# The delta net's triangular systems: substituted in two groups of eight instead of sixteen at once

## The chip, the cores and the metric

The kernel runs on one core of a Trainium2 chip. The metric is the device time of one execution in microseconds (us), the median of several runs. Five engines work side by side: TensorE (PE) multiplies matrices and transposes into PSUM, VectorE (DVE) and ScalarE (ACT) work element by element on SBUF and PSUM, GpSimd (POOL) on SBUF alone, and SyncE (SP) issues the loads.

## The reference, cut to what matters

The reference is a block with a mixer and a mixture of experts, and after it four layers: attention with forget gates, gated linear attention, the gated delta net, and attention again. The change is in the delta net, `gdn_mixer`, with 256 tokens, 8 value heads of 128, 4 key heads and chunks of 64 tokens:

```python
qkv = jax.nn.silu(causal_conv(qkv, conv_w))
q = l2_norm(q) * d ** -0.5; k = l2_norm(k)      # each repeated for two heads
...
tri = jnp.where(strict, (kb @ k.T) * decay, 0.0) + jnp.eye(64)
u = triangular_solve(tri, vb)
w = triangular_solve(tri, kb * exp(gc))
...   # then a scan over the chunks with u, w and the queries
```

For each head and chunk a unit lower triangular system of 64 has to be solved. The kernel makes the inverse of `tri` itself.

## The kernel before

**Layout.** Function `gdn` does the layer. Two chunks stand in one 128x128 tile, so 8 heads by 2 token tiles give 16 "systems" of 128x128; U (line 1526) holds their strict triangles. Four systems are worked on at a time, in a PSUM tile of 512 columns: group g4 = 0 to 3 has heads 2 g4 and 2 g4 + 1. Groups 0 and 1, the first eight systems, need key heads 0 and 1 (unit 2) and query unit 0; groups 2 and 3 need units 3 and 1.

**Units.** The columns of the input weights are taken in units of 256 (`unit`, line 1497: 2 and 3 keys, 0 and 1 queries, 4 to 7 values) and two for the gate z (2048, of 512 columns, and 2560). The raw weights, 1 MB a unit, are loaded into a ring of six buffers (pool `ring`, tag "w"); ACT rounds each half unit (line 247) and DVE takes the rest (line 248), so that a product is done in three passes, and PE does 48 matmuls for a unit (line 277; line 298 where tokens are the rows). The end of a dense product traces the load and the split of the next unit (`ahead`, line 261). The product stands in PSUM (pool `pd`, four tiles); `conv_silu` copies it into one buffer "pad" on DVE (352), multiplies by four taps on ACT (356) and DVE (360), and applies silu (363, 365). `l2` normalises keys and queries: squares on ACT, sums on PE (1510), the inverse root on POOL, transposes (1520), a multiply on DVE (1522). `systems` makes U from them (1550 to 1561).

**The inverse.** `compact` picks the 8x8 diagonal blocks of four systems into `own`. `substitute` inverts all of them by forward substitution: their coefficients are widened (1601: a part on ACT, a part on POOL) and transposed into PSUM (1604), and then seven rows are made one after another, each by a multiply and a reduce on DVE (1609, 1610) that read the coefficients from PSUM. The result is transposed back (1612), spread into block diagonal tiles T and, flipped by PE (1581), V = its transpose. Three levels of doubling (8 to 16, 32, 64) follow: `lower` multiplies U by T (1636) and masks it into X (1642), `update` multiplies X by V or V by X and adds (1654, 1655), `flipped` copies the flipped T into V (1660). In `update` the level decides which. One loop does the twelve steps (three levels by four groups) with a lag, so that four groups are under way.

**What sets the order.** A planner orders each engine's instructions when the kernel is built, by its own costs: of those ready it takes the one that is first in the program. `issue_after` adds an order on one engine alone. Two ties matter. `conv_silu` issues its copy into pad behind `made[2]`, the last reduce of the substitution, once that is set (line 1499); and `queries` (multiplies on the queries' tiles) behind the last lower step. A tag of a pool gives out a fixed number of buffers: 4 PSUM tiles "ps" for the work above, 4 "pd" for dense products, 2 "cv" for the results of the convolution, and 6 ring buffers "w", of which `zs` (line 1471, the gate z, written from line 1083 on) has one through the whole layer.

After the doubling come `rest`, `upper`, `across` and `lower_half` (1716 to 1736), which solve for the values chunk by chunk, and `result`.

Of the kernel before, what the change touches and what calls it, by code (L numbers as in the profile page):

```python
# [1461 lines left out]
def gdn(s, I, st, hT, cols):  # L1462
# [34 lines left out]
    def unit(u):  # L1497
        pq = first if u == 2 else s.dense(W, 0, 256 * u, T, st.x)
        return s.conv_silu(None, pq, rb2, lambda i, j: cw[:, 16 * j + 2 * u + i:16 * j + 2 * u + i + 1], after=made.get(2))
# [63 lines left out]

    k, q = unit(2), unit(0)
    gate_z(s, st, zs, 0, s.dense_tm(W, 2048, st.x))
    kn, qn = l2(k, q)
    k = unit(3)
    systems(0, kn, qn)
    q = unit(1)
    kn, qn = l2(k, q)  # L1570
    systems(1, kn, qn)

    def sys4(t, g4):
        return t[:, 4 * g4:4 * g4 + 4]
# [15 lines left out]

    def substitute():

        nc.vector.tensor_tensor(own, own, s.eye8[:, None, :].to_broadcast([P, 16, 8]), OP.add)
        t = s.tmp.tile([P, 16, 8], F32, tag="junk", name="rows8", bufs=1)
        nc.vector.tensor_copy(t, s.eye8[:, None, :].to_broadcast([P, 16, 8]))
        pts = [s.ps.tile([P, 512], F32, name="ps") for _ in range(2)]
        for c, n in enumerate((4, 3)):
            wide = s.tmp.tile([P, 4, 16, 8], F32, tag="kq"[c], name="wide")  # L1600
            (nc.scalar.copy, nc.gpsimd.tensor_copy)[c](
                wide[:, :n], own[:, :, 4 * c + 1:4 * c + 1 + n].rearrange("p a i -> p i a")[:, :, :, None].to_broadcast([P, n, 16, 8]))
            for i in range(n):
                nc.tensor.transpose(pts[c][:, i * P:(i + 1) * P], wide[:, i].rearrange("p a c -> p (a c)"), s.ident)
        for i in range(1, 8):
            at = (i - 1) % 4 * P
            m = pts[i // 5][:, at:at + P].rearrange("p (n j) -> p n j", j=8)[:, :, :i + 1]
            x = s.tmp.tile([P, 16, 8], F32, tag="E", name="terms")
            nc.vector.tensor_tensor(x[:, :, :i + 1], m, t[:, :, :i + 1], OP.mult)
            made[2] = nc.vector.tensor_reduce(t[:, :, i], x[:, :, :i + 1], AX.X, OP.add).ins  # L1610
        pt = s.ps.tile([P, 512], F32, name="ps")
        nc.tensor.transpose(pt[:, :P], t.rearrange("p n i -> p (n i)"), s.ident)
        nc.scalar.copy(own.rearrange("p a c -> p (a c)"), pt[:, :P])

# [7 lines left out]

    X, last = {}, [None]

    def halves(x, lev):

        x = x.rearrange("p a (n c) -> p a n c", c=16 << lev)
        return x[:, :, :, :8 << lev], x[:, :, :, 8 << lev:]

    def lower(i):  # L1630

        lev, g4 = divmod(i, 4)
        t = sys4(Tm, g4)
        pt = s.ps.tile([P, 512], F32, name="ps")
        for a in range(4):
            nc.tensor.matmul(pt[:, a * P:(a + 1) * P], U[:, 2 * g4 + a // 2, (a % 2) * P:(a % 2 + 1) * P], t[:, a],  # L1636
                             start=True, stop=True)
        X[i] = s.tmp.tile([P, 4, P], F32, tag="kq"[i % 2], name="X")
        xl, xr = halves(X[i], lev)
        nc.gpsimd.memset(xr, 0.0)  # L1640
        nb = P // (16 << lev)
        last[0] = nc.vector.tensor_tensor(
            xl, halves(pt.rearrange("p (a t) -> p a t", a=4), lev)[0],
                                s.below[:, lev, :nb][:, None, :, None].to_broadcast([P, 4, nb, 8 << lev]), OP.mult).ins

    def update(i):

        lev, g4 = divmod(i, 4)
        t, v, x = sys4(Tm, g4), sys4(Vm, g4), X[i]
        l, m, out, side = (v, x, t, 0) if lev < 2 else (x, v, v, 1)  # L1650
        out = halves(out, lev)[side]
        pt = s.ps.tile([P, 512], F32, name="ps")
        for a in range(4):
            nc.tensor.matmul(pt[:, a * P:(a + 1) * P], l[:, a], m[:, a], start=True, stop=True)  # L1654
        nc.vector.tensor_tensor(out, out, halves(pt.rearrange("p (a t) -> p a t", a=4), lev)[side], OP.add)

    def flipped(i):
        lev, g4 = divmod(i, 4)
        if lev < 2:
            nc.scalar.copy(halves(sys4(Vm, g4), lev)[1], halves(flip(sys4(Tm, g4)), lev)[1])  # L1660
# [13 lines left out]

    for g4 in range(4):
        compact(g4)
    substitute()
    v_dense(0)
    v_dense(1)
    for g4 in range(4):  # L1680
        spread(g4)
    v_turn(0)
    for i in range(12 + 3):
        if i < 12:
            lower(i)
        if 0 <= i - 2 < 12:
            update(i - 2)
        if 0 <= i - 3 < 12:
            flipped(i - 3)
        if i in (0, 5):  # L1690
            v_dense(2 + i // 5)
        if i in (3, 7, 10):
            v_turn((3, 7, 10).index(i) + 1)
        if i >= 4 and i < 12 and i % 2 == 0:
            with s.tc.issue_after(last[0]):
                queries((i - 4) // 2)

# [260 lines left out]
```

## Time and profile before

| what | value |
|---|---|
| median of three runs (lowest, highest) | 1293.36 us (1290.65, 1295.31) |
| the profiled execution: its own time, its span | 1291.23 us, 1289.6 us |
| PE, DVE, ACT busy, share of the span | 88%, 46%, 38% |
| delta net: first dense products about, substitution, end of the results | 970 us, 1050 to 1065 us, 1113 us |
| one split on DVE (line 248), mean | 1.22 us |

All times in rows are microseconds from the span's start; the page's engine shares are averages over stages that are bound in different ways. A busy time is from the start of an instruction to its end; a matmul starts while the one ahead of it is still in the pipeline, so the distance of starts is the price of one more. What a stage is limited by is read from the waits in it.

### The profile page before, as it was taken

Reading aid. Unit: us, or ns where it says so; the run is one execution under the profiler, and the core shown is the slowest. Engines: PE = TensorE matmul, PEld = TensorE weight load, DVE = VectorE, ACT = ScalarE, POOL = GpSimd, SP = SyncE. Lnnn points to the kernel's source line nnn. Section 1 sums busy time; section 2 is a strip of 40 time slices with the busy share of each in tenths; the row PEclk is TensorE's granted clock in tenths of the full one; section 3 lists DMA queues with packets and bytes.
Section 4 is the critical chain, followed back from the end, with each engine's and each line's share of the span. In section 5 each row is a group of like instructions: output and inputs, shape, how many; then the busy total and the mean of one; then the engine's idle time right before and its main releaser. Section 6 shows DMA issues by size and latency. Waiting matters only on the chain.

```text
span 1289.6 us, 18973 instructions
## 1 busy us (share of the span) xinstructions
PE 1134.1 (88%) x7458; PEld 845.0 (66%) x7459; DVE 589.9 (46%) x1136; ACT 491.4 (38%) x996; POOL 137.6 (11%) x406
## 2 busy tenths in 40 slices
PE   5999999996778677777777999999999969999998
PEld 4998999741323131322314788989688959897887
DVE  3976776410101010110104565757467777666554
ACT  4554454210101010000104567656455533356763
POOL 2000632000000000000000332010001110012310
PEclk8999999998899898999989999999999979999999
DMA  6843647799999999999999553454335420165620
GB/s 226 290 134 99 191 159 283 280 421 425 421 424 424 425 424 424 425 425 424 425 424 317 171 164 131 166 165 153 112 109 170 138 76 2 34 165 168 158 98 33
DMA packets 126903, 312.72 MB, mean 242 GB/s; under 512 B 7559, under 2 KB 72842, under 8 KB 109530
## 3 DMA queue, kind: packets, MB, share of 16 engines
q1 hardware_dynamic: 126458, 311.26, 65.5%
q8 instruction: 60, 0.98, 0.3%
q0 software_dynamic: 352, 0.20, 0.1%
q14 instruction: 33, 0.27, 0.1%
HBM read 310.39 MB, written 1.05 MB: 242 GB/s over the span
## 4 chain that ended last, share of the span: by engine, by line
PE 39%; DMA 25%; DVE 3%; ACT 2%; issue 1%; POOL 1%; SPq 0%; DVEq 0%; ACTq 0%
PE pd L298 19%; DMA we<-in_w_down 12%; PE pd L277 9%; DMA we<-in_w_gate 6%; DMA we<-in_w_up 6%; DMA w<-in_fox_w_in 2%; DVE wl L248 1%; PE ps L1654 1%; PE ps L1193 1%; PE ps L1581 1%; PE ps L1636 1%; ACT wh L247 1%; PE ps L1211 1%; PE pd L969 1%; DVE cv L360 0%
## 5 line engine op out<-in xcount | busy, mean ns | idle before, releaser
L277 PE MATMUL pd<-x,wh 128*128 128x256 f32 x1744 | 327.6, 288 | 2.3 <-DVE x L161 1.2
L248 DVE TENSOR_TENSOR wl<-w,wh 128x1024 fp32r<-128x1024 f32 (+1 forms) x206 | 251.2, 1223 | 119.0 <-ACT wh L247 117.6
L247 ACT CAST wh<-w 128x1024 fp32r<-128x1024 f32 (+1 forms) x206 | 214.5, 1046 | 203.2 <-PE pd L277 103.8
L277 PEld LDWEIGHTS pd<-x,wh 128*128 128x128 f32 x1744 | 276.7, 194 | 5.5 <-DVE x L161 2.1
L298 PE MATMUL pd<-wh,x 128*128 128x512 f32 (+3 forms) x896 | 249.5, 367 | 6.9 <-ACT x L160 2.4
L277 PE MATMUL pd<-x,wl 128*128 128x256 f32 x872 | 248.8, 287 | 0.8 <-DVE wl L248 0.8
L969 PE MATMUL pd<-we,xt 128*32 128x512 f32 x1012 | 173.2, 681 | 71.9 <-DMA we<-in_w_up 50.6
L298 PEld LDWEIGHTS pd<-wh,x 128*128 128x128 f32 x896 | 159.7, 190 | 33.8 <-ACT wh L247 3.8
L277 PEld LDWEIGHTS pd<-x,wl 128*128 128x128 f32 x872 | 168.7, 194 | 1.6 <-DVE wl L248 1.3
L969 PEld LDWEIGHTS pd<-we,xt 128*32 128x32 f32 x1012 | 40.5, 122 | 195.7 <-DMA we<-in_w_up 86.8
L298 PE MATMUL pd<-wl,x 128*128 128x512 f32 (+3 forms) x448 | 158.3, 366 | 1.5 <-DVE wl L248 1.4
L993 PE MATMUL pd<-we,sq 128*32 128x512 f32 x512 | 98.2, 624 | 27.6 <-DMA we<-in_w_down 21.7
L298 PEld LDWEIGHTS pd<-wl,x 128*128 128x128 f32 x448 | 84.2, 190 | 15.6 <-DVE wl L248 2.9
L1005 DVE TENSOR_TENSOR hT<-hT,ps 128x512 f32<-128x512 f32 x32 | 22.0, 687 | 149.3 <-PE ps L1004 149.3
L993 PEld LDWEIGHTS pd<-we,sq 128*32 128x32 f32 x512 | 24.7, 112 | 94.0 <-issue 45.0
L982 DVE SCALAR_TENSOR_TENSOR cv<-cv,rslot,pd 128x512 f32<-128x512 f32 x8 | 6.0, 747 | 130.9 <-PE pd L969 130.9
L99 POOL TENSOR_SCALAR rq_y<-rs_v 128x8 int32<-128x8 int32 (+2 forms) x24 | 6.4, 266 | 522.8 <-DVE rs_v L192 440.0
L987 ACT COPY sq<-ps 128x512 f32<-128x512 f32 x8 | 4.7, 585 | 149.8 <-PE ps L985 149.8
L999 ACT COPY ys<-pd 128x512 f32<-128x512 f32 x16 | 9.3, 586 | 120.7 <-PE pd L993 120.7
L1316 POOL MEMSET at<- 128x1024 f32 x1 | 1.0, 951 | 434.7 <-PE pd L993 434.7
L980 DVE SCALAR_TENSOR_TENSOR cv<-th,pd 128x512 f32<-128x512 f32 x8 | 5.5, 688 | 85.8 <-ACT th L978 85.8
L978 ACT ACTIVATE th<-pd,rslot 128x512 f32<-128x512 f32 x8 | 5.5, 687 | 90.3 <-PE pd L969 51.3
(492 smaller groups left out, 1374.3 us busy)
## 6 DMA issues: line engine op xcount, KB each, us to landing
we<-in_w_down SPq DMA_DIRECT2D x46, 1024.0 KB, 14.8
we<-in_w_up SPq DMA_DIRECT2D x45, 1024.0 KB, 16.0
we<-in_w_gate SPq DMA_DIRECT2D x43, 1024.0 KB, 14.5
w<-in_fox_w_in SPq DMA_DIRECT2D x30, 1024.0 KB, 6.8
w<-in_w_in SPq DMA_DIRECT2D x22, 1024.0 KB, 7.7
we<-in_w_up SPq DMA_DIRECT2D x38, 512.0 KB, 14.2
we<-in_w_down SPq DMA_DIRECT2D x36, 512.0 KB, 15.8
we<-in_w_gate SPq DMA_DIRECT2D x34, 512.0 KB, 15.6
```

The source lines that it names most:

```text
L247: nc.scalar.copy(h, v[:, k:k + m])
L248: nc.vector.tensor_tensor(l, v[:, k:k + m], h, OP.subtract)
L277: nc.tensor.matmul(acc[:, c], w[k][:, cs], x[:, k, p], start=start and c == 0 and at == 0 and i == 0, stop=stop and at == KC - 1 and i == ...
L298: nc.tensor.matmul(acc[j], x[:, k, p, ts], w[k], start=k == order[0] and i == 0 and (n != T or j == 0), stop=k == order[-1] and i == 2, sk ...
L969: mm = nc.tensor.matmul(out[32 * j:32 * j + 32], xt[:, k, 32 * j:32 * j + 32], w[name, 4 * q + j, k // 4][k % 4], start=k == 0, stop=k == ...
L993: mm = nc.tensor.matmul(py[h][32 * j:32 * j + 32], at[:, f, 32 * j:32 * j + 32], w["w_down", 4 * q + j, f // 2][f % 2][:, 512 * h:512 * h ...
L1005: nc.vector.tensor_tensor(hT[:, 2 * u:2 * u + 2], hT[:, 2 * u:2 * u + 2], pt.rearrange("p (i t) -> p i t", i=2), OP.add)
L1193: nc.tensor.transpose(pt[:, (2 * i + j) * P:(2 * i + j + 1) * P], n4[w, j][:, 2 * o + i], s.ident)
L1211: nc.tensor.matmul(pl[:, P:384], q[:, P:], k, start=False, stop=False, skip_group_check=True)
L1581: nc.tensor.transpose(pt[:, a * P:(a + 1) * P], x[:, a], s.ident)
L1636: nc.tensor.matmul(pt[:, a * P:(a + 1) * P], U[:, 2 * g4 + a // 2, (a % 2) * P:(a % 2 + 1) * P], t[:, a], start=True, stop=True)
L1654: nc.tensor.matmul(pt[:, a * P:(a + 1) * P], l[:, a], m[:, a], start=True, stop=True)
```

## The change

The sixteen systems are substituted eight at a time. `substitute(u)` takes one half of `own`, with 64 partitions (8 systems by 8 columns); ACT makes the whole wide copy, and ACT copies the transposed coefficients from PSUM into SBUF, from where the seven rows read them. The substitution of the first eight stands before unit 1 in the program, and the convolution of unit 1 is now behind its last reduce. The first eight are doubled, level by level with two groups in turn, after the second eight's substitution in the program and before its result is transposed back (`substituted`). The second eight follow in the same way, with the value units between. The buffers X of the doubling, which were in tags "k" and "q" for each step anew, are one tile of the ring "w" for the whole layer; a half of it also holds the wide copy and the coefficients of the substitution.

```diff
--- before.py
+++ after.py
@@ -1561,139 +1561,160 @@
+    room = s.ring.tile([P, KC * WIDE], F32, tag="w", name="X")[:, :2048].rearrange("p (u g a t) -> p u g a t", u=2, g=2, a=4)
+    X = [room[:, 0], room[:, 1]]
+    sys4x = lambda g4: X[g4 // 2][:, g4 % 2]
...
+    def substitute(u):
+
+        mine = own[:, 8 * u:8 * u + 8]
+        nc.vector.tensor_tensor(mine, mine, s.eye8[:, None, :].to_broadcast([P, 8, 8]), OP.add)
+        t = s.tmp.tile([64, 16, 8], F32, tag="junk", name="rows8", bufs=1)
+        nc.vector.tensor_copy(t, s.eye8[:64, None, :].to_broadcast([64, 16, 8]))
+        flat = X[u].rearrange("p g a t -> p (g a t)")
+        wide = flat[:, 576:].rearrange("p (i a c) -> p i a c", i=7, a=8)
+        nc.scalar.copy(wide, mine[:, :, 1:].rearrange("p a i -> p i a")[:, :, :, None].to_broadcast([P, 7, 8, 8]))
+        rows_of = lambda i: flat[:64, (i - 1) * P:i * P]
+        for at, n in ((0, 4), (4, 3)):
+            pt = s.ps.tile([P, 512], F32, name="ps")
+            for i in range(n):
+                nc.tensor.transpose(pt[:64, i * P:(i + 1) * P], wide[:, at + i].rearrange("p a c -> p (a c)"), s.ident)
+            nc.scalar.copy(flat[:64, at * P:(at + n) * P], pt[:64, :n * P])
+        for i in range(1, 8):
+            m = rows_of(i).rearrange("p (n j) -> p n j", j=8)[:, :, :i + 1]
+            x = s.tmp.tile([64, 16, 8], F32, tag="E", name="terms")
+            nc.vector.tensor_tensor(x[:, :, :i + 1], m, t[:, :, :i + 1], OP.mult)
+            made[2] = nc.vector.tensor_reduce(t[:, :, i], x[:, :, :i + 1], AX.X, OP.add).ins
+        return t
+
+    def substituted(u, t):
+        mine = own[:, 8 * u:8 * u + 8]
+        pt = s.ps.tile([P, 512], F32, name="ps")
+        nc.tensor.transpose(pt[:, :64], t.rearrange("p n i -> p (n i)"), s.ident[:64, :64])
+        nc.scalar.copy(mine.rearrange("p a c -> p (a c)"), pt[:, :64])
...
+    def lower(lev, g4):
+
+        t = sys4(Tm, g4)
...
+        xl, xr = halves(sys4x(g4), lev)
+        nc.gpsimd.memset(xr, 0.0)
+        nb = P // (16 << lev)
+        last[0] = nc.vector.tensor_tensor(
...
+    def update(lev, g4):
+
+        t, v, x = sys4(Tm, g4), sys4(Vm, g4), sys4x(g4)
...
+    def double(u, lev):
+        for step in (lower, update, flipped):
+            for g4 in (2 * u, 2 * u + 1):
+                step(lev, g4)
+
+    def pick(u):
+        compact(2 * u)
+        compact(2 * u + 1)
+
+    def end(u):
+        spread(2 * u)
+        spread(2 * u + 1)
     k, q = unit(2), unit(0)
     gate_z(s, st, zs, 0, s.dense_tm(W, 2048, st.x))
     kn, qn = l2(k, q)
     k = unit(3)
     systems(0, kn, qn)
+    pick(0)
+    t = substitute(0)
     q = unit(1)
+    substituted(0, t)
     kn, qn = l2(k, q)
+    end(0)
     systems(1, kn, qn)
...
-    def substitute():
-
-        nc.vector.tensor_tensor(own, own, s.eye8[:, None, :].to_broadcast([P, 16, 8]), OP.add)
-        t = s.tmp.tile([P, 16, 8], F32, tag="junk", name="rows8", bufs=1)
-        nc.vector.tensor_copy(t, s.eye8[:, None, :].to_broadcast([P, 16, 8]))
-        pts = [s.ps.tile([P, 512], F32, name="ps") for _ in range(2)]
-        for c, n in enumerate((4, 3)):
-            wide = s.tmp.tile([P, 4, 16, 8], F32, tag="kq"[c], name="wide")
-            (nc.scalar.copy, nc.gpsimd.tensor_copy)[c](
-                wide[:, :n], own[:, :, 4 * c + 1:4 * c + 1 + n].rearrange("p a i -> p i a")[:, :, :, None].to_broadcast([P, n, 16, 8]))
-            for i in range(n):
-                nc.tensor.transpose(pts[c][:, i * P:(i + 1) * P], wide[:, i].rearrange("p a c -> p (a c)"), s.ident)
-        for i in range(1, 8):
-            at = (i - 1) % 4 * P
-            m = pts[i // 5][:, at:at + P].rearrange("p (n j) -> p n j", j=8)[:, :, :i + 1]
-            x = s.tmp.tile([P, 16, 8], F32, tag="E", name="terms")
-            nc.vector.tensor_tensor(x[:, :, :i + 1], m, t[:, :, :i + 1], OP.mult)
-            made[2] = nc.vector.tensor_reduce(t[:, :, i], x[:, :, :i + 1], AX.X, OP.add).ins
-        pt = s.ps.tile([P, 512], F32, name="ps")
-        nc.tensor.transpose(pt[:, :P], t.rearrange("p n i -> p (n i)"), s.ident)
-        nc.scalar.copy(own.rearrange("p a c -> p (a c)"), pt[:, :P])
...
-    def lower(i):
-
-        lev, g4 = divmod(i, 4)
-        t = sys4(Tm, g4)
...
-        X[i] = s.tmp.tile([P, 4, P], F32, tag="kq"[i % 2], name="X")
-        xl, xr = halves(X[i], lev)
-        nc.gpsimd.memset(xr, 0.0)
...
-    def update(i):
-
-        lev, g4 = divmod(i, 4)
-        t, v, x = sys4(Tm, g4), sys4(Vm, g4), X[i]
...
-    for g4 in range(4):
-        compact(g4)
-    substitute()
+    pick(1)
+    t = substitute(1)
     v_dense(0)
+    for lev in range(3):
+        double(0, lev)
     v_dense(1)
-    for g4 in range(4):
-        spread(g4)
+    substituted(1, t)
     v_turn(0)
-    for i in range(12 + 3):
-        if i < 12:
-            lower(i)
-        if 0 <= i - 2 < 12:
-            update(i - 2)
-        if 0 <= i - 3 < 12:
-            flipped(i - 3)
-        if i in (0, 5):
-            v_dense(2 + i // 5)
-        if i in (3, 7, 10):
-            v_turn((3, 7, 10).index(i) + 1)
-        if i >= 4 and i < 12 and i % 2 == 0:
+    end(1)
+    double(1, 0)
+    v_dense(2)
+    v_turn(1)
+    for lev in (1, 2):
+        double(1, lev)
+        for g4 in (2 * lev - 2, 2 * lev - 1):
             with s.tc.issue_after(last[0]):
-                queries((i - 4) // 2)
+                queries(g4)
+        if lev == 1:
+            v_dense(3)
+            v_turn(2)
+    v_turn(3)
```

The functions `flip`, `compact`, `spread`, `halves`, `v_dense` and `v_turn` only move up, unchanged; `update` and `flipped` take level and group where they took a running number.

## Rows read from the trace of the kernel before

**Rows 1.** Waits of PE, 1000 to 1100: total us, times, longest us

```profile
PE ps L1604 <- ACT wide L1601: 4.9, 1, 4.9
PE ps L1612 <- DVE rows L1610: 3.3, 1, 3.3
PE ps L1672 <- DVE cv L365: 1.9, 1, 1.9
PE ps L1581 <- DVE TV L1618: 1.3, 1, 1.3
PE ps L1581 <- DVE TV L1655: 0.6, 1, 0.6
```

**Rows 2.** Timeline of PE: start us, us, instructions, count

```profile
1059.64 3.65 PE L1581 MATMUL ps<-ident,TV 128*128 128x128 f32 x16 [1.25 <-DVE TV L1618]
...
1065.71 2.84 PE L1636 MATMUL ps<-TV,U 128*128 128x128 f32 x24
...
1077.16 0.60 PE L1581 MATMUL ps<-ident,TV 128*128 128x128 f32 x4
1077.59 1.06 PE L1636 MATMUL ps<-TV,U 128*128 128x128 f32 x8
```

**Rows 3.** Stretches: length, busy us (instructions) of PE, PEld, DVE, ACT, POOL; clock, DMA share, GB/s

```profile
1009.70:1029.00 19.30, 19.30 (x155) 18.08 (x154) 16.61 (x33) 11.69 (x25) 0.91 (x3) 1.00 0.33 110
...
1041.30:1052.80 11.50, 6.31 (x42) 4.66 (x40) 9.22 (x18) 5.93 (x16) 0.55 (x2) 0.88 0.48 95
1052.80:1065.20 12.40, 5.88 (x24) 4.82 (x24) 10.25 (x28) 4.70 (x10) 1.08 (x4) 0.56 0.00 0
1065.20:1093.80 28.60, 27.84 (x246) 27.49 (x247) 23.13 (x63) 8.85 (x20) 2.49 (x8) 1.00 0.00 1
```

**Rows 4.** Timelines of ACT, DVE and SP's queue, 945 to 985

```profile
979.40 0.84 ACT L1082 ACTIVATE th<-pd,rh 128x256 f32<-128x256 f32 x2 [3.47 <-DVE gx L1477]
...
982.89 1.98 ACT L247 CAST wh<-w 128x1024 fp32r<-128x1024 f32 x2
...
979.90 0.79 DVE L1083 SCALAR_TENSOR_TENSOR zs<-th,pd 128x256 f32<-128x256 f32 x2 [0.27 <-ACT th L1082]
...
945.47 14.57 SPq L229 DMA_DIRECT2D w<-in_gdn_w_in  x3
```

**Rows 5.** Timeline of DVE, 1051 to 1064

```profile
1051.83 0.29 DVE L1595 TENSOR_TENSOR own<-own,eye 128x128 f32<-128x128 f32 x1
1053.98 0.19 DVE L1609 TENSOR_TENSOR terms<-ps,rows 128x32 f32<-128x32 f32 x1 [1.86 <-PE ps L1604]
...
1057.24 0.29 DVE L1609 TENSOR_TENSOR terms<-ps,rows 128x128 f32<-128x128 f32 x1
...
1057.77 0.68 DVE L352 TENSOR_TENSOR pad<-pd,rstd_b 128x512 f32<-128x512 f32 x1
...
1061.21 2.46 DVE L360 SCALAR_TENSOR_TENSOR cv<-pad,gconv_half,cv 128x256 f32<-128x256 f32 x6
```

**Rows 6.** Timeline of ACT, the wide copy

```profile
1052.15 0.62 ACT L1601 COPY wide<-own 128x512 f32<-128x512 f32 x1 [3.08 <-DVE own L1595]
```

**Rows 7.** Timeline of DVE, 1028 to 1043

```profile
1028.03 0.69 DVE L365 SCALAR_TENSOR_TENSOR cv<-th,cv 128x512 f32<-128x512 f32 x1
...
1033.01 1.22 DVE L248 TENSOR_TENSOR wl<-w,wh 128x1024 fp32r<-128x1024 f32 x1
1034.15 1.11 DVE L1591 TENSOR_REDUCE own<-sq 128x32 f32<-128x512 f32 x1
...
1041.94 0.69 DVE L1522 TENSOR_TENSOR k<-ps,cv 128x512 f32<-128x512 f32 x1 [1.13 <-PE ps L1520]
```

**Rows 8.** Groups of DVE, 1053 to 1092: count, busy us, mean ns, idle before

```profile
L1642 DVE TENSOR_TENSOR X<-ps,below 128x256 f32<-128x256 f32 x12 | 5.0, 416 | 3.6 <-PE ps L1636 2.8 <-issue 0.8
```

**Rows 9.** Timeline of DVE, the first eight's way to the keys

```profile
996.28 0.68 DVE L365 SCALAR_TENSOR_TENSOR cv<-th,cv 128x512 f32<-128x512 f32 x1
...
1012.95 0.68 DVE L1522 TENSOR_TENSOR k<-ps,cv 128x512 f32<-128x512 f32 x1
```

More of the change, by code (lines that the diff above doesn't have):

```diff
@@ L1562, in systems @@
             qkp[g4] = prod[1]
[L1564 to L1571, printed above, removed]
+    room = s.ring.tile([P, KC * WIDE], F32, tag="w", name="X")[:, :2048].rearrange("p (u g a t) -> p u g a t", u=2, g=2, a=4)
+    X = [room[:, 0], room[:, 1]]
+    sys4x = lambda g4: X[g4 // 2][:, g4 % 2]
     def sys4(t, g4):
@@ L1621, in spread @@
         nc.scalar.copy(v, flip(t))
-    X, last = {}, [None]
+    last = [None]
     def halves(x, lev):
@@ L1655, in update, with flipped @@
         nc.vector.tensor_tensor(out, out, halves(pt.rearrange("p (a t) -> p a t", a=4), lev)[side], OP.add)
-    def flipped(i):
-        lev, g4 = divmod(i, 4)
+    def flipped(lev, g4):
         if lev < 2:
@@ L1673, in v_turn @@
         nc.scalar.copy(v[:, :, 256 * u:256 * u + 256], pt.rearrange("p (j c) -> p j c", j=2))
-    for g4 in range(4):
-        compact(g4)
-    substitute()
+    def double(u, lev):
[8 more added lines that the diff above has]
+        spread(2 * u + 1)
+    k, q = unit(2), unit(0)
+    gate_z(s, st, zs, 0, s.dense_tm(W, 2048, st.x))
+    kn, qn = l2(k, q)
+    k = unit(3)
+    systems(0, kn, qn)
+    pick(0)
+    t = substitute(0)
+    q = unit(1)
+    substituted(0, t)
+    kn, qn = l2(k, q)
+    end(0)
+    systems(1, kn, qn)
+    pick(1)
+    t = substitute(1)
     v_dense(0)
+    for lev in range(3):
+        double(0, lev)
     v_dense(1)
-    for g4 in range(4):
-        spread(g4)
+    substituted(1, t)
     v_turn(0)
-    for i in range(12 + 3):
-        if i < 12:
-            lower(i)
-        if 0 <= i - 2 < 12:
-            update(i - 2)
-        if 0 <= i - 3 < 12:
-            flipped(i - 3)
-        if i in (0, 5):
-            v_dense(2 + i // 5)
-        if i in (3, 7, 10):
-            v_turn((3, 7, 10).index(i) + 1)
-        if i >= 4 and i < 12 and i % 2 == 0:
-            with s.tc.issue_after(last[0]):
-                queries((i - 4) // 2)
+    end(1)
[5 more added lines that the diff above has]
+        for g4 in (2 * lev - 2, 2 * lev - 1):
+            with s.tc.issue_after(last[0]):
+                queries(g4)
[3 more added lines that the diff above has]
+    v_turn(3)
     lo, hi = slice(0, 64), slice(64, P)
```

## The prediction, made before the changed kernel was run

> **What bounds the kernel now.** I read TensorE's (PE's) waits in the delta net's layer first [rows 1]. Four lie around the substitution: 4.9 us until the coefficients are widened, 3.3 us for the chain of small DVE instructions, 1.3 us for the spreading, 1.9 us for a convolved v unit; a fifth, 0.6, follows in the doubling. Together 12.0 us. Then PE's instructions there [rows 2]: 16 flips take 3.65 us, 0.228 each, while later four of them take 0.43, start to next start, 0.11 each. [...]
>
> [...] From 1009.7 to 1029.0 PE is busy throughout [rows 3], 155 matmuls at 0.12, most of them dense products of the four v units (48 each, 192 x 0.12 = 23 us in all); these run on to 1041.3. From 1065.2 to 1093.8 PE is the bound again: the doubling goes in steps of 0.9 us (lower products of four systems, eight matmuls; 24 take 2.84), as long for as many updates, and 0.43 (flips) [rows 2]. DVE is full almost as long: 10.25 of 12.4 us, then 23.13 of 28.6 [rows 3].
>
> **An order that the trace shows.** Tiles of one tag seem to be given out in the order of their first writes in the program, and what needs a later tile is queued behind. Two places. The two casts that begin the 512-wide unit start at 982.89, back to back, though ACT had stood idle for 3.47 us and the unit's loads were issued before 960.1 (of the layer's twelve loads the last ten lie in the trace behind 945; the first three of these are unit 0 and the two of this unit): they come 3.0 us after the first write of zs, at 979.90, which lies ahead of these loads in the same tag "w" [rows 4]. The lower products of the first group, whose operands are there after the first spread, start only at 1065.71, behind the transposes of v unit 0, for which PE waited 1.9 us, and whose PSUM tile is the earlier one [rows 1, 2].
>
> **The change part by part.**
>
> *The second substitution.* From the first multiply to the pad copy behind the last reduce the chain takes 3.8 us [rows 5]. If halving the partitions halved its instructions, two chains would cost what one does; if partitions don't count, 7.6. The multiplies grow with the elements of a partition (0.19 us for 32, 0.29 for 128), which stay as they are, so I take 7.6: DVE +3.8.
>
> *The copies of the coefficients.* ACT makes one wide copy, 0.62 as for 512 elements [rows 6] (POOL did the other part beside it), and two copies out of PSUM, at most that much each; the first, 0.6, is on the path of each substitution. The multiplies now read SBUF: 128 elements take 0.29 from PSUM, and the addition of 128 elements in SBUF takes 0.29 too [rows 5], so nothing is won. [...]
>
> *Eight more transposes*: 8 x 0.11 = 0.9 us of PE. Spreads are the same in all; POOL's copy is gone, which costs and gives nothing.
>
> *X in the ring of weights.* X is first written by the wide copy of the first substitution, and this stands ahead of the loads of all four v units in tag "w". By the first place their casts then come 3.0 us after X's first write, the first matmul 1.0 later. When is that write? Before, the last compaction of the first eight ended at 1035.2 [rows 7], with the convolution of unit 1 (3.9: pad 0.6, six terms of 0.41, the end 0.6 [rows 5, 7]) and four splits of 1.1 among it, which now come later: 1035.2 - 3.9 - 4.4 = 1026.9. PE's parts of that chain also no longer stand behind dense products. I take 1024 (bounds 1022 and 1027), so dense work again at 1028. From 1009.7 until then PE has the first eight systems (6.3 by the second eight, PE's busy time from 1041.3 to 1052.8 [rows 3]) and some 2.7 of sums and transposes, 9.0 of 18.3. The early hole: 9.3 us (bounds 6 and 13). The clock may fall in it, as it did behind 1052.8, and the first matmuls behind it run slow: 1.5 us (0 to 3). The transfers themselves stay hidden: they run 20 us ahead of the casts [rows 4], and one buffer less leaves that at some 15.
>
> *The convolution of unit 1* is tied behind the first chain on DVE. Write of X 1024, two copies and four transposes 2.0, chain 3.8, two splits of 1.1 between: tied end 1032. The convolution with its activations takes 6: 1038, instead of 1028.7 [rows 7]. From there to the normalised keys took 13.2 us [rows 7]; ACT and DVE are less full now, so I take 10.5 (bounds 9 and 16). Keys at 1048.5 instead of 1041.9, and all behind them 6.6 later: the second transposes at 1059.4 instead of 1052.8, the second tie, behind which the v convolutions wait, at 1065.5 instead of 1057.8 (copy 0.6, first doublings among the chain).
>
> *PE from 1028.* Dense 23.0, second systems, sums, flips and transposes 9.0, clock 1.5: full until 1061.5, so the late hole is covered. Then the first eight's doubling, six pairs of 1.8 and two of 0.87: 12.5. The transposition that ends the second substitution stands behind it by the order of PSUM tiles; after it come ACT's copy, spread and flips, a bubble of 1.5, flips 0.9; then again 12.5. With two groups in turn in place of four a flip waits for the sum just before it: 2.5 in all (1 to 5). With the v transposes, 1.8: 1061.5 + 12.5 + 1.5 + 0.9 + 12.5 + 2.5 + 1.8 = 1093.2, against 1093.8 before.
>
> *DVE from 1065.5.* Of the 33.4 us from 1052.8 to 1093.8 [rows 3], the chain (3.8), the first eight's spread (1.2) and their doubling (12 instructions like the 12 of one line, 5.0 [rows 8]) are done by then: 23.4, until about 1089. PE ends the place, where it ended before.
>
> **The sum**, as PE's lost time. Before: 12.0 + 2.6 = 14.6. After: early hole 9.3, clock 1.5, bubble and stalls 4.0, transposes 0.9, less 1.0 for upper products of the first eight that may go early: 14.7. The late hole is exchanged for an early one. The profiled execution took 1291.2 us with a span of 1289.6; the median of three runs is 1293.4, 2.1 above it. Adding 0.1 to the median: 1293.5. The bounds of the single terms reach from -6 to +8 but will hardly fall together; this case alone has 1289 to 1298.
>
> **The rivals.**
>
> *Faster.* The v units are not held back by X, and the first doubling gets in while the keys of the second eight are made. Then PE has neither hole: 14.6 goes, 0.9 + 2.5 comes, 1293.4 - 11.2 = 1282. For it: 23 us of dense work and 12.5 of doubling are more than either hole. Against it: the two places above; by the order of PSUM tiles the first doubling stands behind the second eight's transposes, wherever the dense work goes. Between lie shorter early holes, 1284 to 1289.
>
> *Slower: PE runs dry a second time.* It decides when the second transposes come later than PE's backlog lasts, 1061.5; I have them at 1059.4, only 2.1 earlier. The first eight's way from convolution to keys took 16.0 us [rows 9]. If the second way takes that, in place of 10.5, the transposes come at 1064.9: 3.4 us of standing still, 1.5 more for the clock behind it, and the tie at 1071 leaves DVE until 1094.4, at PE's heels: 1293.5 + 5 = 1298.5. For it: each step of that way queues behind dense work, as it did. Against it: fewer splits and convolutions share DVE and ACT.
>
> *Only the order of weights is misread.* Then PE is full until 1042, and empty until keys at 1048.5 and transposes at 1059.4, since the doubling is behind these: the hole merely moves, 1293 to 1296, and counts with my forecast.
>
> **How the numbers follow.** 0.3% of 1293.4 is 3.9 us, about what a measurement can tell from no change. Holes exchanged, no change: 0.41. Faster, by the first rival or a part of it: 0.26. Slower, by the second or by the upper bounds of hole and stalls: 0.33. For 8 in 10 the low end goes to 1284, which leaves out the full gain of the first rival (0.11), and the high end to 1302, past the second's price (0.08 left out).
>
> **What would show it.** In the stretches of after: PE idle for some 9 us between 1010 and 1029; casts of v unit 0 only behind the first wide copy; keys of the second eight near 1048, second transposes near 1059; PE without a gap over 1 us from 1029 to 1059; doubling's end near 1093. The forecast is wrong if dense products of v units run before the first eight's coefficients are widened, if first doublings run before the second systems, or if the second tie falls after 1068.

## The result, and the profile after

The changed kernel takes 1304.36 us (median of 5 runs, 1303.16 to 1307.97), the kernel before 1293.36 (5 runs); the ratio is 1.0095, 95% interval 1.0071 to 1.0119. It is slower, and above the 1302 at which the forecast's range ends. The profiled execution has a span of 1301.6 us, 12.0 more than before's.

First, where the 12.0 lie. The stretches of both kernels (before first; columns as in [rows 3]), from the first matmul of line 1486, ahead of all that the change touches, to the end of the doubling, and from there to the next layer's dense products (the second L277 that waits for x):

```profile
999.21:1093.77 94.56, 82.09 (x657) 77.81 (x656) 73.36 (x165) 39.55 (x80) 12.25 (x39) 0.93 0.25 74
1093.77:1121.45 27.68, 26.17 (x214) 23.14 (x213) 17.49 (x55) 10.76 (x33) 0.00 (x0) 1.00 0.05 9
```

```profile
1001.79:1103.49 101.70, 86.16 (x665) 79.79 (x664) 75.37 (x179) 41.26 (x85) 9.74 (x38) 0.93 0.21 68
1103.49:1132.28 28.79, 26.98 (x216) 23.09 (x213) 17.98 (x56) 11.27 (x34) 0.00 (x0) 1.00 0.23 45
...
1020.00:1030.00 10.00, 2.50 (x9) 1.57 (x9) 7.19 (x21) 5.96 (x13) 0.32 (x1) 0.63 0.00 1
1030.00:1040.00 10.00, 8.98 (x54) 8.78 (x55) 9.39 (x18) 3.50 (x6) 0.31 (x1) 0.69 0.37 115
...
1060.00:1070.00 10.00, 6.99 (x56) 6.17 (x55) 7.58 (x15) 5.55 (x12) 0.00 (x0) 1.00 0.33 105
```

Up to the doubling's end it takes 7.1 us more: PE stands still for 15.5 in place of 12.5, and is busy for 4.1 longer; the results take 1.1 more. Together 8.25; I call this stretch the place, 122.24 us before, 130.49 after. Of the other 3.8, 2.6 came ahead of line 1486 and 1.2 behind the place; they are told at the end.

Beside [rows 1], the waits of PE after, 1000 to 1130 (total us, times, longest):

```profile
PE ps L1601 <- ACT X L1596: 8.7, 2, 5.7
PE ps L1576 <- DVE TV L1653: 2.6, 2, 2.1
PE pd L277 <- ACT wh L247: 1.6, 1, 1.6
PE pd L277 <- DVE wl L248: 1.4, 1, 1.4
PE pd L1737 <- ACT v L1670: 0.7, 1, 0.7
```

The chain, the spreading and the v unit have gone from the list; the coefficients are waited for twice. The timeline of PE after shows when (start us, us, instructions, count, idle before):

```profile
1013.23 1.03 PE L1520 MATMUL ps<-ident,fl 128*128 128x128 f32 x8
1014.70 0.91 PE L1550 MATMUL ps<-k 128*128 128x128 f32 x6 [0.44 <-DVE k L1522]
...
1025.59 1.70 PE L1601 MATMUL ps<-ident,X 128*64 128x128 f32 x7 [5.65 <-ACT X L1596]
1028.86 0.80 PE L277 MATMUL pd<-x,wh 128*128 128x256 f32 x2 [1.56 <-ACT wh L247]
1031.02 0.58 PE L277 MATMUL pd<-x,wl 128*128 128x256 f32 x1 [1.37 <-DVE wl L248]
...
1051.88 1.03 PE L1520 MATMUL ps<-ident,fl 128*128 128x128 f32 x8
...
1055.42 0.83 PE L1550 MATMUL ps<-k 128*128 128x128 f32 x6
...
1060.20 0.83 PE L1550 MATMUL ps<-k 128*128 128x128 f32 x6
...
1068.26 0.95 PE L1601 MATMUL ps<-ident,X 128*64 128x128 f32 x7 [3.01 <-ACT X L1596]
1069.05 1.17 PE L1636 MATMUL ps<-TV,U 128*128 128x128 f32 x9
...
1083.38 0.27 PE L1613 MATMUL ps<-ident,rows 64*128 64x64 f32 x1
...
1086.33 1.95 PE L1636 MATMUL ps<-TV,U 128*128 128x128 f32 x16
...
1098.18 1.09 PE L1576 MATMUL ps<-ident,TV 128*128 128x128 f32 x8 [2.11 <-DVE TV L1653]
```

The early hole is there (5.65 + 1.56 + 1.37, the products behind it at a clock of 0.50, rows at the end), PE stands still a second time before the second transposes, and each doubling is in one piece, the first from 1069.05, the second from 1086.33 to 1103.49.

### The profile page after: what moved, and what is told of

It is laid out like the page before. It is cut to its first block, busy times and chain, and to the rows that moved or that the text cites. A ratio compares the mean times of both kernels' runs of the same rounds, so it can differ in the third digit from the quotient of the medians.

```text
span 1301.6 us, 18995 instructions
## 1 busy us (share of the span) xinstructions
PE 1140.7 (88%) x7466; PEld 847.5 (65%) x7467; DVE 592.6 (46%) x1152; ACT 493.3 (38%) x1002; POOL 134.5 (10%) x405
## 4 chain that ended last, share of the span: by engine, by line
PE 39%; DMA 24%; DVE 5%; ACT 2%; issue 1%; POOL 1%; SPq 0%; DVEq 0%; ACTq 0%
PE pd L298 20%; DMA we<-in_w_up 10%; PE pd L277 9%; DMA we<-in_w_down 7%; DMA we<-in_w_gate 6%; DMA w<-in_fox_w_in 2%; PE pd L969 2%; DVE wl L248 1%; DVE cv L360 1%; ACT wh L247 1%; PE ps L1193 1%; PE ps L1211 1%; PE ps L1636 0%; PE ps L1410 0%; PE ps L1231 0%
## 5 line engine op out<-in xcount | busy, mean ns | idle before, releaser
L277 PE MATMUL pd<-x,wh 128*128 128x256 f32 x1744 | 328.3, 288 | 4.6 <-ACT wh L247 2.4
L277 PEld LDWEIGHTS pd<-x,wh 128*128 128x128 f32 x1744 | 277.2, 194 | 8.2 <-ACT wh L247 3.3
L277 PE MATMUL pd<-x,wl 128*128 128x256 f32 x872 | 248.7, 287 | 2.6 <-DVE wl L248 2.6
L277 PEld LDWEIGHTS pd<-x,wl 128*128 128x128 f32 x872 | 168.9, 194 | 3.9 <-DVE wl L248 3.5
## 6 DMA issues: line engine op xcount, KB each, us to landing
we<-in_w_gate SPq DMA_DIRECT2D x43, 1024.0 KB, 14.6
```

The source lines that it names most:

```text
L277: nc.tensor.matmul(acc[:, c], w[k][:, cs], x[:, k, p], start=start and c == 0 and at == 0 and i == 0, stop=stop and at == KC - 1 and i == ...
```

## The experiments

All are edits of the changed kernel unless it is said otherwise. "Place" is the stretch defined above, read in each run's one profile: e15, with the same work there as the kernel before, has its 122.24 to 0.01 us, while the medians also hold what happens outside the place. Differences of places under some 2 us are not read: the clock granted behind the second doubling's last wait was 0.83 to 0.86 for 10 us in some of these executions (e3, e4, e5, e9, e11, e12) and 1.00 in others, which is worth up to 1.7 us (10 us times the 0.17 that are missing at 0.83). The runs were taken in four rounds, in which the median of the kernel before lay between 1291.2 and 1294.3; each ratio is to the kernel before of its own round.

| run | median us | ratio to before, 95% interval | place us |
|---|---|---|---|
| before / changed | 1293.4 / 1304.4 | 1.0095 [1.0071, 1.0119] | 122.24 / 130.49 |
| e1_early_write | 1307.3 | 1.0118 [1.0091, 1.0144] | 133.81 |
| e2_early_write_levels | 1310.9 | 1.0143 [1.0117, 1.0170] | 138.30 |
| e3_no_tie | 1306.0 | 1.0106 [1.0082, 1.0129] | 134.19 |
| e5_level0 | 1306.3 | 1.0104 [1.0079, 1.0129] | 133.42 |
| e6_first_tie | 1307.1 | 1.0120 [1.0091, 1.0149] | 134.95 |
| e7_first_tie_levels | 1308.8 | 1.0113 [1.0087, 1.0140] | 134.10 |
| e8_queries_late | 1304.0 | 1.0079 [1.0052, 1.0106] | 133.97 |
| e4_from_psum | 1304.0 | 1.0074 [1.0048, 1.0100] | 129.47 |
| e9_second_keys_first | 1301.2 | 1.0074 [1.0051, 1.0097] | 130.91 |
| e10_second_systems_first | 1296.9 | 1.0030 [1.0014, 1.0046] | 122.66 |
| e11_systems_first_tie | 1297.5 | 1.0038 [1.0023, 1.0052] | 124.56 |
| e12_systems_first_tie_level | 1298.5 | 1.0039 [1.0017, 1.0061] | 123.70 |
| e13_x_outside | 1297.4 | 1.0030 [1.0012, 1.0048] | 121.85 |
| e14_systems_first_psum | 1295.8 | 1.0034 [1.0019, 1.0050] | 123.67 |
| e15_before_spare | 1292.9 | 1.0009 [0.9992, 1.0026] | 122.24 |
| e16_chain_first | 1299.0 | 1.0056 [1.0037, 1.0076] | 123.89 |

**First round: are the two holes the cause?** e1 lets the weights go by an early write into columns of X that nothing reads; e2 also puts two levels of the first doubling ahead of the second substitution; e3 unties the convolution of unit 1; e5 moves one level alone. e1, and the lines that e2 adds to it:

```diff
     pick(0)
+    nc.gpsimd.memset(full[:, 2048:2056], 0.0)
     t = substitute(0)
...
     pick(1)
+    double(0, 0)
+    double(0, 1)
     t = substitute(1)
```

and e3:

```diff
-        return s.conv_silu(None, pq, rb2, ..., after=made.get(2))
+        return s.conv_silu(None, pq, rb2, ..., after=made.get(2) if u > 3 else None)
```

> The changed kernel, with one small early write into X's tile (eight columns that nothing reads), which can run long before the first wide copy. Theory (X holds back the weights; then PE runs dry a second time): the dense products of the four v units now run while the first coefficients are made, and the stretch from 1013 to 1029, which lost some 9 us of PE and 3 to 4 of clock, is filled. What runs there is missing later: since the first doubling still stands behind the second transposes by the order of PSUM tiles, the standing still before the second transposes grows from 3.0 to some 6 to 9 us. The second systems no longer queue behind dense products and splits, so these transposes come near 1060 in place of 1068.3. Time 1297 (1294 to 1300). Rival A (the two chains and the doubling in pairs set the time, whatever the dense work does): transposes stay at 1068, time 1304 +- 2. Rival B (one buffer of weights fewer makes loads late): time 1304 or more, dense products waiting for loads.

> As the run with the early write, and the first two of the three levels of the first doubling are written ahead of the second substitution (the third behind it), so that their PSUM tiles come before those of the second transposes. Theory: the early stretch is filled by dense products and the standing still before the second transposes by some 8.5 us of doubling; the third level and the v transposes cover the second chain in part. Time 1290 (1286 to 1295), at or below the kernel before. Rival A (DVE is the bound once doubling and the second systems share it): the second chain comes as much later as the doubling comes earlier, and the time is that of the run with the early write alone, +- 2. Rival B (the hold of the weights costs nothing): 1301 to 1304.

> The changed kernel, with the convolution of unit 1 no longer tied behind the last reduce of the first chain (the v units' ties stay). Theory: the second keys come some 2 to 5 us earlier and the second systems with them, so the standing still of 3.0 us before the second transposes goes, and the early one stays as it is: 1301 (1299 to 1303). Rival (the tie is the main cause, by delaying all that follows the second keys): the whole doubling ends 6 to 9 us earlier, 1295 to 1298.

> The changed kernel, with the first level alone of the first doubling written ahead of the second substitution, weights held as before. Theory: some 4 us of doubling fill the 3.0 us in which PE stood still before the second transposes, and the early standing still stays: 1301 (1299 to 1303). Rival (DVE, busy 9.2 and 10.0 of 10 us from 1070 to 1090, is the bound there): nothing is won, 1304 +- 1.5; PE's standing still moves into the doubling.

All four missed (e1's rival A came nearest): each did to its hole what was meant, and none made the place shorter. It is 3.3 us longer in e1 and 7.8 in e2; in e3 and e5 it is 3.7 and 2.9 longer, of which the lower clock can be 1.7 each, and in e5 as much again (0.83 was also granted from 1080 to 1090). e1 shows why. PE's timeline there:

```profile
1014.31 1.03 PE L1520 MATMUL ps<-ident,fl 128*128 128x128 f32 x8
...
1018.42 0.83 PE L1550 MATMUL ps<-k 128*128 128x128 f32 x6
...
1034.45 0.93 PE L1602 MATMUL ps<-ident,X 128*64 128x128 f32 x7
...
1041.09 0.34 PE L1614 MATMUL ps<-ident,rows 64*128 64x64 f32 x1 [4.04 <-DVE rows L1608]
...
1055.91 1.97 PE L1520 MATMUL ps<-ident,fl 128*128 128x128 f32 x8 [4.61 <-POOL fl L109]
...
1069.50 1.70 PE L1602 MATMUL ps<-ident,X 128*64 128x128 f32 x7 [4.74 <-ACT X L1597]
```

PE is full until 1037, but the first systems now queue behind the freed dense products and their splits: 4.1 us from the first keys' transposes to the first products in place of 1.5, 20.1 to the first coefficients in place of 12.4. Later it stands still three times for 4 to 5 us, each time for a step of one chain: first rows, second keys, second coefficients. e3's second standing still is gone too (its backlog lasts longer), at the price of a longer early one, 8.8. In e5 the late hole is filled, and PE waits 3.9 us for the first v convolution instead. Filling PE moves the holes. So the theory that they set the time fell.

**Second round: DVE's load, or the way from step to step?** e6 ties the v units' convolutions behind the first chain alone (`made.setdefault(2, ...)`), e7 does so in e2, e8 moves the sixteen multiplies of the queries behind the doubling, e4 leaves ACT's copies out.

> The changed kernel, with the convolutions of the four v units tied behind the first chain of substitution (as that of unit 1 is), no longer behind the second. My first theory, that PE's two holes alone set the time, has fallen: with either hole filled nothing was won. Theory D (after the second chain all four convolutions meet the doubling on DVE, which is 26.2 of 28.7 us busy from 1074.6 to 1103.3): two of them move to 1040 to 1068, where DVE was busy 4 to 7 of 10, and the doubling ends 3 to 6 us earlier: 1299 (1297 to 1301). Theory S (the way from the second keys over the second chain to the second doubling is the bound, a chain of small steps on four engines): convolutions on that way only lengthen it, 1304 +- 2 or more.

> The run with the early write into X and two levels of the first doubling ahead of the second substitution (1310.9 us, where PE waited 5.5 us for the first v convolution), with the convolutions of the v units tied behind the first chain. Theory D: this wait goes and the later convolutions no longer crowd the second doubling: 1302 (1299 to 1305). Theory S: the second keys, some 4 us later than in the changed kernel, and the second chain behind them still set the end: 1307 or more.

> The changed kernel, with all sixteen multiplications of the queries behind the last level of the doubling; eight of them had stood on DVE ahead of the additions of T for which PE waited 2.1 us. Theory D and S alike: this wait goes, and the sixteen (some 5.7 us of DVE) run while PE makes the upper and lower products: 1302 (1301 to 1303.5). Rival (DVE is the bound up to the results, whatever the order): they are missing there, 1304 +- 1.5 or more.

> The changed kernel without ACT's copies of the coefficients from PSUM to SBUF; the multiplications read PSUM, as in the kernel before. The two copies stand on the way of each chain (1.2 us from the first transposes to the first multiply), and a multiply from PSUM takes some 0.01 us more: if the way over both chains sets the time, 1 to 2 us are won, 1302.5 (1301.5 to 1303.5). [...] Rival (the copies are hidden): 1304.

Spreading DVE's load (theory D) wins nothing in e6 and 4 of e2's 8 us in e7, where it ended a wait of 5.5 us for the first v convolution. In e8 the wait of 2.1 us is gone and the doubling ends 2.2 us earlier, but behind it the granted clock falls in the profiled execution (stretches as above):

```profile
1100.00:1110.00 10.00, 9.07 (x70) 7.87 (x69) 7.51 (x25) 2.50 (x6) 0.00 (x0) 0.96 0.44 88
1110.00:1120.00 10.00, 10.00 (x45) 8.72 (x44) 3.37 (x8) 0.92 (x4) 0.00 (x0) 0.53 0.12 23
```

At 0.53 the 10 us there hold 4.7 us of lost time; without it the place would be 129.3, some 1 us shorter than the changed kernel's. The median, 0.4 below it, shows no more. Without the copies the place is 1.0 us shorter in e4 (up to 2.7 with its lower clock allowed for), and the median 0.4; the last multiply takes 0.28 us from SBUF in the changed kernel and 0.28 from PSUM in e4, both with 64 partitions (0.29 from PSUM with 128, in the kernel before [rows 5]). All of it, with e8's clock allowed for, fits theory S, that a chain of steps sets the time, but only e9 and e10 put it to the test.

**Third round: shorten the way.** e9 (from e1) makes the second keys ahead of the first substitution; e10 also its systems, before the first substitution ends. e11 is e10 with e6's tie, e12 is e11 with the first level ahead of the second substitution. The lines that e10 moves:

```diff
+    q = unit(1)
+    kn, qn = l2(k, q)
     pick(0)
...
     t = substitute(0)
-    q = unit(1)
+    systems(1, kn, qn)
     substituted(0, t)
-    kn, qn = l2(k, q)
     end(0)
-    systems(1, kn, qn)
     pick(1)
```

> The run with the early write into X (1307.3 us), with unit 1 and the normalising of the second keys written ahead of the first substitution, so that its convolution is no longer tied either. Theory S (two chains in series set the time: the second keys can only come behind the first chain, the second chain behind these, and only one doubling lies behind that): the second keys come as early as in the kernel before, some 10 us earlier than in the run with the early write, and the second transposes some 6 to 8 earlier, since flips and second systems still queue behind the first chain. 1299 (1296 to 1301). Rival P (the parts themselves cost it: two chains, copies, transposes, doubling by pairs): 1305 or more.

> As the run with the second keys first, and the second systems are also written ahead of the end of the first substitution, so that PE makes them beneath the first chain. Theory S: the two chains are now in series with one another alone, no longer with keys and systems; the second transposes come right behind the first flips, the second chain lies under the first doubling, and the standing still of the kernel before (9.5 us in three waits behind its second systems) shrinks to some 5: 1289 (1286 to 1293), at or below the kernel before. Rival P: 1300 or more.

> As the run with the second systems first, with the v units' convolutions tied behind the first chain alone. Theory S: they fill DVE while PE runs the first doubling, but stand in the way of the second chain (each piece 0.4 to 0.7 us): within 2 us of the run with the second systems first. Theory D (convolutions crowd the second doubling): 3 us or more below it.

> As the run before it in this list, with the first level of the first doubling ahead of the second substitution. Theory S: PE has that level earlier, while DVE is still at the second coefficients, at the price of a second chain that starts some 3 to 4 us later and has less doubling above it: within 2 us of the run before it. If the second coefficients are late there (DVE), this run is 2 to 3 us faster than it.

From e1 to e9 the median falls by 6.1 us, from e9 to e10 by 4.3 (by the ratios 5.7 each; the place by 2.9 and 8.3, or some 4.6 and 6.6 with e9's lower clock allowed for), with the same arithmetic. e11 and e12 came out as theory S had it, within 2 us of e10 and of e11. In us from the first transposes of line 1520, by the starts in PE's timelines (the doubling by its end):

| | before | changed | e1 | e9 | e10 |
|---|---|---|---|---|---|
| second keys' transposes | 29.4 | 38.7 | 41.6 | 29.4 | 29.4 |
| last transposes of coefficients | 40.9 | 55.0 | 55.2 | 50.5 | 44.9 |
| doubling ends | 81.8 | 90.3 | 92.3 | 89.4 | 81.1 |

So the loss in the place is the way of the second eight behind the first chain, not the split's own work (rival P). The place of e10 is within 0.4 us of that of the kernel before, not below it, as I had expected (1289 in all, 1296.9 measured). Its rows, PE and then DVE, show what is left:

```profile
1053.32 0.28 PE L338 MATMUL ps<-negq,identb 128*128 128x256 bf16 x1
1059.11 0.34 PE L1614 MATMUL ps<-ident,rows 64*128 64x64 f32 x1 [5.50 <-ACT X L1597]
1060.57 1.94 PE L1577 MATMUL ps<-ident,TV 128*128 128x128 f32 x8 [1.12 <-DVE TV L1620]
```

```profile
1049.77 0.18 DVE L1607 TENSOR_TENSOR terms<-X,rows 64x32 f32<-64x32 f32 x1
1049.87 0.54 DVE L1554 TENSOR_TENSOR kk<-ps,strict 128x384 f32<-128x384 f32 x1
...
1054.90 0.24 DVE L1607 TENSOR_TENSOR terms<-X,rows 64x96 f32<-64x96 f32 x1
1055.07 0.41 DVE L1560 TENSOR_TENSOR U<-Qd,kk 128x256 f32<-128x256 f32 x1
...
1058.68 0.28 DVE L1608 TENSOR_REDUCE rows<-terms 64x16 f32<-64x128 f32 x1
```

PE waits for the first chain's last reduce (the view names a copy that was long done); the chain takes 9.2 us (3.8 before), as the second systems' products and compactions stand between its steps.

**Fourth round: the rest.** e13 takes X out of the ring and leaves out the copies, e14 the copies alone, both in e10. e15 is the kernel before, with an unused tile in one buffer of the ring. e16 (from e13) ties those products of the second systems on DVE behind the chain and moves one level ahead:

```diff
+                with s.tc.issue_after(made[2]) if u else nullcontext():
                     nc.vector.tensor_tensor(U[:, h, :T], Qd[:, h], prod[0][:, :T], OP.mult)
                     nc.vector.tensor_tensor(U[:, h, T:], Qx[:, h], prod[0][:, T:], OP.mult)
```

> As the run with the second systems first, with X and the widened coefficients in the temporary tiles of keys and queries, as in the kernel before, not in the ring of weights, and with no copies of the coefficients (the multiplications read PSUM). If X's place in the ring costs the 1.2 us behind the results and the copies some 1 us on the first chain's way: 1294.5 (1293 to 1296). If only the copies count: 1296 and still 1.2 us more behind the results. If neither: 1297.

> As the run with the second systems first, without the copies of the coefficients, X still in the ring. Theory: the first chain begins 1.2 us earlier and so does what follows it; the second is under the first doubling. 1296 (1295 to 1297). Rival (copies hidden): 1297.

> The kernel before, with one buffer of the ring of weights taken by an unused tile from before its substitution until its doubling ends (two small writes of POOL, nothing else). If a buffer fewer costs time (loads or casts that come later, here or behind the results): 1 to 3 us more than the kernel before, with the 1.2 us behind the results. If it costs nothing: the same within 1 us.

> As the run with X outside the ring, with the products U of the second systems on DVE tied behind the first chain's last reduce, and the first level of the first doubling ahead of the second substitution. Theory: the first chain takes 4 to 5 us in place of 9.2, first flips and first level run some 4 us earlier, beneath the second systems on DVE, and the doubling ends 3 to 5 us earlier than in the run with X outside the ring: 1291 (1288 to 1293). Rival (DVE, 27 of 30 us busy from 1070 to 1100 in the run with the second systems first, is the bound of the whole place): the same as the run with X outside the ring, +- 1.5.

A buffer fewer costs nothing that median or place show (e15: ratio 1.0009, place 122.24). X outside the ring and no copies (e13) leave the place within 0.8 us of e10's, and what leaving the copies out does has no one sign (-1.0 in e4, +1.0 in e14; e14's median lies in its forecast, but its ratio, 1.0034, is not below e10's 1.0030): neither is where the rest lies. In e16 (1291 expected, 1299.0 measured) the chain is done 4.3 us earlier than in e13 (5.1 than in e10), and two other waits take its place:

```profile
1053.85 0.27 PE L1613 MATMUL ps<-ident,rows 64*128 64x64 f32 x1
1056.19 1.23 PE L1576 MATMUL ps<-ident,TV 128*128 128x128 f32 x8 [2.07 <-DVE TV L1619]
...
1073.40 0.27 PE L1613 MATMUL ps<-ident,rows 64*128 64x64 f32 x1
1077.33 0.63 PE L1670 MATMUL ps<-ident,cv 128*128 128x128 f32 x4 [3.66 <-DVE cv L365]
```

The transposes of v unit 0 wait for its convolution, which was tied behind the second chain. No version that was run beats the kernel before.

## Why the prediction was wrong

The forecast was "holes exchanged, no change"; the time went beyond its range, by the mechanism of the slower rival (PE runs dry a second time), though not by the leg that the rival gave for it. In the prediction's own scale (the times after less 2.6, by which line 1486 starts later, 1001.79 to 999.21):

- *The order* was read rightly. The v units' casts come right behind the first coefficients' copies, the first doubling starts right behind the second transposes (1068.26, 1069.05), and the second substitution is transposed back only behind the first doubling (1083.38), though its chain had ended at 1074.64. e1 shows the hold by X directly: with the early write dense products run on behind the first keys' transposes (1014.31, products from 1015.10), in the changed kernel they begin again at 1028.86.
- *The early hole*: 9.3 forecast, 8.6 measured. X's first write 1024, measured 1022.4; dense work again at 1028, measured 1026.3 and 1028.4; the first tie 1032, 1031.5; the end of unit 1's convolution 1038, 1038.2.
- *The clock* was under-sized: 1.5 forecast. The loss, busy time by what the clock lacks, is 2.50 x 0.37 + 8.98 x 0.31 = 3.7 in the two stretches shown. The 2.6 that the sum has for the kernel before, in its 14.6, is an estimate (5.88 us busy at a granted 0.56 [rows 3], 5.88 x 0.44): no run shows it as a loss by itself, and what the stretches show in its place is PE standing still for 12.5 us up to the doubling's end, at a mean granted clock of 0.93. (One reading of the prediction was off without weight: the parts given for unit 1's convolution add up to 3.7, not 3.9.)
- *The step that failed* is "all behind them 6.6 later: the second transposes at 1059.4", by which the way from second keys to second transposes stayed at 10.9. The keys came at 1049.9 (1048.5 forecast), the transposes at 1065.7, 15.75 behind them. Convolution to keys, the leg that the rival had at 16.0, took 11.7 (10.5 forecast). Before, the dense products were over when the keys came, and the first second products started 0.75 behind these; now they start 2.9 behind them, with 15 dense products ahead, 19 more stand between the two sets of second products (1055.42, 1060.20), and three splits among DVE's steps (1055.50, 1061.24, 1066.25). So the backlog, which ended at 1062.7 (1061.5 forecast), ran out 3.0 us too early, and the second tie came at 1072.0, not 1065.5: past the 1068 given as what would refute the forecast.
- *Bubble and stalls*: 4.0 forecast; from 1070 to 1110 PE stands still for 3.6. By starts they were under-sized even so: from the first doubling's start to the second's end the forecast has 31.7 us, the trace 34.4 (1069.05 to 1103.49), 0.4 of the difference for upper products.
- *Upper products that go early*: the 1.0 credited was hardly there, eight of them come ahead of the doubling's end in place of six.

For the step that failed, the first second products before (PE), and the second keys after (DVE):

```profile
1042.69 0.94 PE L1550 MATMUL ps<-k 128*128 128x128 f32 x6 [0.35 <-DVE k L1522]
```

```profile
1052.51 0.69 DVE L1522 TENSOR_TENSOR k<-ps,cv 128x512 f32<-128x512 f32 x1 [0.41 <-PE ps L1520]
```

With 3.7 for the clock, 3.0 for the second standing still and the measured sizes of the other terms the sum is about 5 us above its 14.7. By starts the 7.1 up to the doubling's end close: the first doubling began 4.95 later than forecast (1066.45, not 1061.5), the doublings took 2.7 longer, and the forecast had ended 0.6 ahead of the kernel before. The rival's 1298.5 had the second standing still and 1.5 for the clock, and lacked the rest: the place grew by 8.25, and 3.8 came outside it, where the prediction had looked for nothing.

The deeper error is the account itself. It counts PE's lost time and so suggests that filling a hole wins its length. The first four runs refute that, and e9 and e10 show what holds in its place: the place is as long as the way from first keys over two chains to the last doubling, and a hole is where PE waits for that way. The change put the first chain ahead of the second keys on it.

**Open.** Ahead of the place and behind it the changed kernels lose time with the same instructions. The waits of ACT for the first load of the first attention layer's weights, and of PE for a cast behind the place, in the kernel before, the changed one, e13 and e15, in this order:

```profile
ACT wh L247 <- DMA w<-in_fox_w_in: 2.8, 1, 2.8
...
PE pd L298 <- ACT wh L247: 0.8, 1, 0.8
```

```profile
ACT wh L247 <- DMA w<-in_fox_w_in: 4.4, 1, 4.4
...
PE pd L298 <- ACT wh L247: 2.2, 1, 2.2
```

```profile
ACT wh L247 <- DMA w<-in_fox_w_in: 4.9, 1, 4.9
...
PE pd L298 <- ACT wh L247: 2.2, 1, 2.2
```

```profile
ACT wh L247 <- DMA w<-in_fox_w_in: 2.9, 1, 2.9
...
PE pd L298 <- ACT wh L247: 0.8, 1, 0.8
```

X in the ring and a buffer fewer are not the cause (e13 has the waits without them, e15 a buffer fewer without the waits). What is wasn't found. In size, 2.6 us ahead and 1.2 behind in the changed kernel, it fits the 0.3% by which e10 and e13, with a place like before's, are still slower. In their profiles the place begins even later, by 5.5 and 6.6 us; 4.0 and 3.3 of these came ahead of 350 us, where the changed kernel and e11 lose 0.3 at most, so this part is not common to the changed kernels.

## What to carry to other kernels

Before counting what a hole in the busiest engine is worth, follow the way of dependent steps through it: with the second half's keys made behind the first half's chain the place was 8.25 us longer here, with its keys and systems made ahead of the end of that chain (e10) 0.4 (no version went below the kernel before, so that a split can pay is not shown); and steps that were quick with no dense products among them were not quick once the work meant to cover them stood in the same queues (from the first keys' transposes to the first products 1.5 us in the changed kernel, 4.1 in e1). Check it by writing the second half's inputs ahead of the first half's chain. A wait that is filled and comes back elsewhere, as the changed kernel's 3.0 us before the second transposes did in e5 as 3.9 for the first v convolution, is a sign of such a way.

## What was not expected of the hardware

The granted clock was 0.53 and 0.50 in stretches in which PE was busy throughout. In e8 it was 0.53 from 1110 to 1120 (rows above), after 10 us in which PE had been busy for 9.07, at 0.96, with no wait over 0.6. In the changed kernel it stays low behind the hole, with PE busy for all of the first stretch:

```profile
1034.00:1036.00 2.00, 2.00 (x11) 2.00 (x11) 1.43 (x4) 0.94 (x3) 0.00 (x0) 0.50 0.99 327
1036.00:1040.00 4.00, 4.00 (x33) 3.80 (x33) 4.00 (x9) 1.86 (x3) 0.00 (x0) 0.97 0.29 91
```

Halving the partitions of the chain's instructions (64 in place of 128) did not shorten the last multiply by more than 0.01 us: from PSUM it takes 0.28 us in e4, 0.29 in the kernel before [rows 5]. Reading SBUF in place of PSUM, with 64 partitions in both, did not shorten it at all: 0.28 us each; the last multiply of the changed kernel, then of e4 (DVE):

```profile
1032.50 0.28 DVE L1606 TENSOR_TENSOR terms<-X,rows 64x128 f32<-64x128 f32 x1
```

```profile
1033.99 0.28 DVE L1607 TENSOR_TENSOR terms<-ps,rows 64x128 f32<-64x128 f32 x1
```
